# A two-layer hybrid decoder trunk in fp32: when the sums of weight blocks are begun

## The chip, the cores and the metric

One NeuronCore of a Trainium2 chip runs the whole program; the other cores are idle. The metric is the device time of one execution in microseconds (us). The kernel before takes 1888.86 us in the median of three runs (1887.78 to 1890.61).

The engines are named as the profile names them: PE (TensorE, matrix multiply), DVE (VectorE), ACT (ScalarE), POOL (GpSimd), and SP (SyncE), which here issues DMAs only. DMAs of SP run on queue q1, those of POOL on queue q0; both are served by the core's 16 DMA engines.

## The reference

Two layers (DEPTH = 2) of width 2048 over 512 tokens. Each layer projects its input once, hands the columns to three groups of heads, gates their output, projects it back and normalises:

```python
h = jnp.einsum('bsd,dn->bsn', x, w_in)
# split into FoX, DSA and memory parts
y_fox = fox_attention(...) * jax.nn.silu(fg)        # 6 heads, log-forget bias
y_dsa = dsa_attention(...) * jax.nn.silu(dg)        # 6 heads, rotary, top 128 keys by an indexer
y_mem = memory_attention(...) * jax.nn.silu(mg)     # 4 heads into 256 memory tokens
y = jnp.einsum('bsn,nd->bsd', jnp.concatenate([y_fox, y_dsa, y_mem], -1), w_out)
return layer_norm(ALPHA * x + y, ln_gain, ln_bias)
```

The indexer has 16 heads of width 64. All arrays are float32.

## The kernel before

**Products.** Every fp32 matrix product is three matmuls: each operand is split into a high part (rounded to fp32r, made by ACT, tile `whi` for weights) and a low part (the rest, made by DVE, tile `wlo`); high x high, high x low and low x high are added up in PSUM. The weights come from a DRAM tensor `wall` in chunks of 128 x 2048 floats (1 MB), each loaded in two halves of 512 KB into tiles `raw` (seven buffers). A half takes 12 matmuls of 512 columns, or 24 in the kinds with a 128-column result.

**Fewer products.** The large projections are computed in blocks of 2 x 2 by a scheme of seven products (`PRODUCTS`, P1, P7, Q4, P2, Q6, Q5, Q3) instead of eight. Some products need a sum or difference of two weight blocks as their right operand. These come about in four ways:
- The product P7 needs T3, the sum of two blocks. For the value stage T3 of the first pair of columns is summed in DRAM beforehand. For the other five pairs both blocks are loaded (`raw` and four quarter tiles `other` per chunk, 2 MB together) and DVE adds them (`pair_w`, L383).
- Q6 and Q4 need T2 and T4, which grow out of T3 and T2 by adding one more block: in the value stage DVE adds a block that is in SBUF anyway (`make_w`, L404), except for Q4 of the last pair, where an accumulating DMA of POOL adds it to the `raw` tile (`grow_w`, L391). The output stage has accumulating DMAs as well.
- Q5 needs T1, summed in DRAM beforehand for all pairs.
- The output stage needs T3 and T1 of its two pairs, summed in DRAM beforehand.

**The sums in DRAM** are what the change is about. A sum of a block of 1 MB is two DMAs of POOL from DRAM to DRAM: one copies the first block, a later one accumulates the second. "A sum" below means one such DMA; there are 44 per layer (4 for T3 and 24 for T1 of the values, 16 for the output), tile `sum`. They read only the weights. Each is preceded by `pool_waits` (L539): ACT (in the value stage) or DVE (elsewhere) copies one column into `mark`, POOL multiplies it into `seen`. As POOL works in order, the DMA is not issued before ACT or DVE has come to that place of its own order.

**The order of the work** is written out by hand. `stream` (L136) lists the chunks; the main loop (L1615) goes through them and issues, per half, the load of the chunk after next (`load_w`), the split three halves ahead, DVE's sum of a loaded pair four halves ahead, and PE's matmuls. A layer has these stages, named in `now[1]`: memory values and keys (`mv`, `mk`; in layer 1 the stage is called "kv"), the small projection and eight indexer chunks ("index"), then six pairs of value columns ("values"), each of ten chunks in this order (the number is the half of the contraction):

```python
VAL_FIRST = (("P1", 0), ("P7", 0), ("P1", 1), ("P7", 1), ("P2", 0), ("Q6", 0), ("Q6", 1), ("P2", 1),
             ("Q4", 0), ("Q4", 1))
```

After each pair come one or two head chunks (`EARLY_AT`: 1, 1, 1, 1, 2, 2), columns of one head's queries or keys. Then Q5 and Q3 of all pairs with the attention heads between their matmuls ("heads"), and the output stage ("out": 14 steps of two chunks, `place_out[0]` holds the step), whose last step begins the normalisation (`next_x`, L1484).

Side work is written as generators. `tick` (L618) advances each that is due; a generator that yields k is advanced again k ticks later. `all_sums` (L590) is one of them, begun after layer 0's small projection with `whole=True`: it takes no part in the tick at the half of a value or output chunk, so it sees one tick per value or output chunk, at its end, and two per chunk of the other kinds. Where the last step of the output stage ends there is one tick more, just as `next_x` is begun. `paced` (L573) sets the distance between sums: one is issued, then `PACE` = 2 ticks pass, 3 in "out", 1 or 2 in turn in "index"; after a sum issued in "kv" or "heads" it waits until that stage is over. `all_sums` begins layer 1's sums when the stage has become layer 1's.

Of the kernel before, what the change touches and what calls it, by code (L numbers as in the profile page):

```python
# [23 lines left out]
DEPTH = 2  # L24
# [14 lines left out]
PACE = 2  # L39
# [96 lines left out]
def stream():  # L136

    wall = all_chunks()
    where = {c: i for i, c in enumerate(wall)}
    out = []  # L140

    def product(kind, l, name, pair, gs=(0, 1)):
        right = PRODUCTS[name][2]
        for g in gs:
            at = lambda step: where[kind, l, 2 * pair + step[1], 2 * step[0] + g]
            if name in GROWN:
                of, step = GROWN[name]
                src = ("grown", (of, at(step)))
            elif kind == "val" and right == "T3" and pair >= IN_DRAM:
                src = ("pair", tuple(at(step) for step in PAIRED[right]))  # L150
            elif isinstance(right, str):
                src = ("sum", (kind, l, right, pair, g))
            else:
                src = ("wall", at(right))
            out.append(({"val": "vs"}.get(kind, kind), l, (name, pair), g, src))

    for i, c in enumerate(wall):
        kind, l, j = c[:3]
        if kind == "out":
            if c == ("out", l, 0, 0):  # L160
                for name, pair in OUT_ORDER:
                    product("out", l, name, pair)
        elif kind == "val":
            if c == ("val", l, 0, 0):
                early = [x for x in wall if x[1] == l and (x[0], x[2]) in HEAD_CHUNKS]
                for order in (VAL_FIRST, VAL_SECOND):
                    for pair in range(PAIRS):
                        for name, g in order:
                            product("val", l, name, pair, (g,))
                        if order is VAL_FIRST:  # L170
                            for _ in range(EARLY_AT[pair]):
                                x = early.pop(0)
                                out.append((*x, ("wall", where[x])))
        elif (kind, j) not in HEAD_CHUNKS:
            out.append((*c, ("wall", i)))
    return out
# [81 lines left out]
def kernel(  # L258
# [26 lines left out]
    def uid(name):  # L285
        count[0] += 1
        return f"{name}_{count[0]}"
# [16 lines left out]
    def bank(name):  # L304
        return psum.tile([P, 512], F32, tag="b", name=uid(name))
# [25 lines left out]
    chunks = stream()  # L331
# [85 lines left out]
    def last_half(i):  # L417

        return i >= len(chunks) - 4
# [119 lines left out]
    def pool_waits():  # L539

        mark, seen = small("mark", 1), small("seen", 1)
        if now[1] == "values":
            nc.scalar.activation(mark, mhalf, AF.Copy)
        else:
            nc.vector.tensor_copy(mark, mhalf)
        nc.gpsimd.tensor_tensor(seen, mark, mhalf, op=ALU.mult)
# [3 lines left out]
    def block(kind, l, pair, g, step):  # L550
        return wall[where[kind, l, 2 * pair + step[1], 2 * step[0] + g]]

    def add_weights(key, src):
        nc.gpsimd.dma_start(sums[key], src, accum_op=ALU.add, max_dma_last_dim=2 * DM)

    def weight_sums(kind, l, names, pairs, some=(0, 1)):

        for name in names:
            for n in some:
                step = SUM_STEPS[name][n]  # L560
                for pair in pairs:
                    for g in range(2):
                        key = (kind, l, name, pair, g)
                        src = block(kind, l, pair, g, step)
                        pool_waits()
                        if n:
                            add_weights(key, src)
                        else:
                            sums[key] = dram.tile([P, DM], F32, name=uid("sum"))
                            nc.gpsimd.dma_start(sums[key], src, max_dma_last_dim=2 * DM)  # L570
                        yield

    def paced(gen):  # L573

        n = 0
        for _ in gen:
            n += 1
            while now[1] in ("kv", "heads"):
                yield 1
            yield {"out": 3, "index": 1 + n % 2}.get(now[1], PACE)  # L580

    def value_sums(l):

        for n in range(2):
            yield from weight_sums("val", l, ("T3",), range(IN_DRAM), (n,))
        for pair in range(PAIRS):
            for n in range(2):
                yield from weight_sums("val", l, ("T1",), (pair,), (n,))

    def all_sums():  # L590


        for l in range(DEPTH):
            yield from paced(value_sums(l))
            yield from paced(weight_sums("out", l, ("T3", "T1"), range(2)))
            while l + 1 < DEPTH and now[0] == l:
                yield 1

    crow_d = [dram.tile([H_FOX, SEQ], F32, name=f"crow{l}") for l in range(DEPTH)]
# [11 lines left out]
    now = (0, "index")  # L611
# [76 lines left out]
    def drain(done):  # L688

        start = clock.at["PE"]  # L690
        while not done():
            advance()
            if not done():
                clock.at["PE"] += 0.2
            assert clock.at["PE"] < start + 100
# [487 lines left out]
    place_out = [0]  # L1183
# [133 lines left out]
    def load_base(name, pair):  # L1317

        for st in range(2):
            r = st + 2 * (name == "Q5")  # L1320
            assert stored[2 * pair + 1, r] == 1
            t = vraw["base", name, pair, st] = slot("vraw")
            nc.sync.dma_start(t, v_d[2 * pair + 1][r * P:(r + 1) * P, :])
# [114 lines left out]
    def load_res(l, st, dc):  # L1438
        z[st, dc] = slot("z")
        src = x_in if l == 0 else x1_d  # L1440
        nc.gpsimd.dma_start(z[st, dc], src[st * P:(st + 1) * P, dc * 512:(dc + 1) * 512])
# [169 lines left out]
    def ahead_of(i):  # L1611
        return i < len(chunks) and chunks[i][0] == "vs" and chunks[i][2][0] in ("Q5", "Q3")

    first = {l: min(i for i, c in enumerate(chunks) if c[1] == l) for l in range(DEPTH)}
    for i, (kind, l, j, col, _) in enumerate(chunks):  # L1615
        late = last_half(i)
        if kind == "out":
            step = OUT_ORDER.index(j)
            name, pair = j
            if step == col == 0:  # L1620
                now, place_out[0] = (l, "out"), 0
            drain(lambda: (PRODUCTS[name][1], 2 * col + 1) in left)
            chain, aname, _, targets = PRODUCTS[name]
            opens = name in ("P1", "P2", "Q6")
            if col == 0:
                if opens:
                    chains[chain, pair] = [bank("z"), bank("z")]
                zs = chains[chain, pair]

                for st, dc in RES_LOADS.get(step, ()):  # L1630
                    load_res(l, st, dc)
                place_out[0] = step
        elif kind == "vs":
            name, pair = j
            aname = PRODUCTS[name][1]
            opens = name in VAL_OPENS
            if col == 0:
                if opens:
                    chains[VAL_CHAIN[name], pair] = [bank("v"), bank("v")]
            elif ahead_of(i + 1) and 2 * chunks[i + 1][2][1] + 1 not in ROWS:  # L1640
                load_base(*chunks[i + 1][2])
            zs = chains[VAL_CHAIN[name], pair]
        elif kind == "mv":
            if col == 0:
                out_ps = {m: bank("v") for m in range(2)}
        else:
            ps = bank("c")
        for h in range(2):
            n = 2 * i + h
# [134 lines left out]
        if kind == "mv" and l > 0:  # L1784
            now = (l, "kv")
        if kind == "small":
            now = (l, "index")
            stored.clear()
            heads_done.clear()
            memT.clear()  # L1790
            left.clear()
            if l == 0:
                begin(all_sums(), whole=True)
            else:
                begin(residual_rows(l), 2, whole=True)
        if kind == "vs":
            now = (l, "heads" if name in ("Q5", "Q3") else "values")
# [11 lines left out]
        if kind == "out" and step == col == 0:  # L1809
            now = (l, "out")  # L1810
# [100 lines left out]
```

## Time and profile before

| | before |
|---|---|
| median of three runs | 1888.86 us (1887.78 to 1890.61) |
| the profiled execution | 1887.66 us |
| its span, first to last instruction | 1885.8 us |
| PE, DVE, ACT, POOL busy, share of the span | 98%, 85%, 57%, 22% |
| DMA moved | 474.20 MB, mean 251 GB/s |
| SP's queue q1, share of 16 engines' span | 49.3% |
| sums in DRAM: number, median us from issue to landing | 88, 10.5 |
| first and last sum of layer 0; of layer 1, begun at (us) | 70.1 and 509.5; 944.7 and 1448.1 |

In a row of the timeline stand the start in us, the duration in us, the engine, the line, the operation, the tiles (written <- read), how many instructions were merged (x2), and in brackets the idle time ahead of it and what ended it. All operations go through one helper, so every row has its line, L242; tiles tell them apart. SPq and POOLq are the rows of issued DMAs, whose duration is that of the issue, not of the transfer. The chain of waits is the work that ended last, followed back from the end; a row has a start, a duration, and what it was. Rows of stretches (a:b) have busy time and instructions of PE, weight loads, DVE, ACT and POOL, then the granted clock of TensorE, the share of the DMA engines and GB/s. PE's matmuls overlap, so PE is shown busy for longer than it works.

### The profile page before, as it was taken

The page shows a single profiled execution, that of the slowest core. Times are in us where ns is not written, and L with a number is a line of the kernel's source. Part 1 is how long each engine was busy: PE and PEld are TensorE (multiplying, and loading weights), DVE is VectorE, ACT ScalarE, POOL GpSimd, SP SyncE. Part 2 cuts the span into 40 slices and gives each one's busy share as a digit, 9 for nine tenths or more (in the row PEclk, how much of TensorE's full clock was granted, in tenths as well). Part 3 has the DMA queues.
Part 4 walks back from the last instruction along what each step waited for, and adds up shares of the span by engine and source line. Part 5 has one row for each costly group of instructions (what it writes and reads, how often), then busy time and mean ns, then how long its engine had stood idle before and what let it go on. Part 6 is the DMA issues. An engine that isn't in the chain of part 4 may idle for free.

```text
span 1885.8 us, 26424 instructions
## 1 busy us (share of the span) xinstructions
PE 1856.2 (98%) x8994; PEld 1576.5 (84%) x8994; DVE 1608.6 (85%) x2565; ACT 1079.9 (57%) x1752; POOL 410.1 (22%) x587
## 2 busy tenths in 40 slices
PE   9999999999999999999999999999999999999997
PEld 8998888887888888888899978888878888888886
DVE  6789789888789987889898998889787898878898
ACT  5776344444357887555476753454353578875553
POOL 0121222121233211240011221211221343113302
PEclk9999999999999999999999999999999999999999
DMA  9986998897999887986579969977979998879866
GB/s 351 294 239 162 300 303 241 298 273 267 251 244 286 257 220 206 265 210 215 190 256 282 264 173 307 324 235 272 290 266 237 248 299 234 220 215 269 239 215 142
DMA packets 230372, 474.20 MB, mean 251 GB/s; under 512 B 76368, under 2 KB 100944, under 8 KB 229980
## 3 DMA queue, kind: packets, MB, share of 16 engines
q1 hardware_dynamic: 176508, 300.48, 49.3%
q0 software_dynamic: 53152, 170.97, 35.5%
q8 instruction: 71, 1.16, 0.2%
q10 hardware_dynamic: 576, 1.05, 0.2%
q14 instruction: 65, 0.53, 0.1%
HBM read 402.15 MB, written 149.97 MB: 293 GB/s over the span
## 4 chain that ended last, share of the span: by engine, by line
PE 77%; DVE 9%; DMA 7%; ACT 3%; issue 2%; SPq 0%; POOL 0%; DVEq 0%; ACTq 0%; POOLq 0%
PE v L242 38%; PE c L242 17%; PE z L242 14%; DMA other<-in_wall_dram 4%; DVE wlo L242 4%; PE po L242 3%; PE ix L242 1%; PE s L242 1%; DMA grown<-sum 1%; PE pt L242 1%; ACT whi L242 1%; DVE raw L242 1%; DMA raw<-in_wall_dram 1%; DVE acc L242 1%; DVE rope L242 1%
## 5 line engine op out<-in xcount | busy, mean ns | idle before, releaser
L242 ACT ACTIVATE whi<-raw 128x1024 fp32r<-128x1024 f32 (+1 forms) x497 | 521.3, 1056 | 457.4 <-PE v L242 196.4
L242 DVE TENSOR_TENSOR wlo<-raw,whi 128x1024 fp32r<-128x1024 f32 (+1 forms) x497 | 601.7, 1217 | 133.0 <-ACT whi L242 130.5
L242 PE MATMUL v<-whi,vxh 128*128 128x512 f32 x768 | 306.7, 399 | 8.2 <-ACT whi L242 4.7
L242 PE MATMUL v<-wlo,vxh 128*128 128x512 f32 x768 | 302.0, 393 | 5.0 <-DVE wlo L242 5.0
L242 PE MATMUL v<-whi,vxl 128*128 128x512 f32 x768 | 301.4, 392 | 0.0
L242 PE MATMUL v<-whi,xh 128*128 128x512 f32 x576 | 224.4, 390 | 0.0
L242 PE MATMUL v<-wlo,xh 128*128 128x512 f32 x576 | 224.2, 389 | 0.0
L242 PE MATMUL v<-whi,xl 128*128 128x512 f32 x576 | 224.1, 389 | 0.0
L242 PE MATMUL c<-xh,whi 128*128 128x512 f32 (+1 forms) x544 | 197.9, 364 | 0.0
L242 PE MATMUL c<-xh,wlo 128*128 128x512 f32 (+1 forms) x544 | 197.8, 364 | 0.0
L242 PE MATMUL c<-xl,whi 128*128 128x512 f32 (+1 forms) x544 | 197.7, 363 | 0.0
L242 POOL TENSOR_TENSOR seen<-mark,mhalf 128x1 f32<-128x1 f32 x88 | 58.3, 662 | 635.6 <-ACT mark L242 452.6
L242 PEld LDWEIGHTS v<-whi,vxh 128*128 128x128 f32 x768 | 145.1, 189 | 40.2 <-ACT whi L242 7.4
L242 PEld LDWEIGHTS v<-wlo,vxh 128*128 128x128 f32 x768 | 145.3, 189 | 35.5 <-DVE wlo L242 8.5
L242 PEld LDWEIGHTS v<-whi,vxl 128*128 128x128 f32 x768 | 145.1, 189 | 30.8
L242 PE MATMUL z<-wlo,yh 128*128 128x512 f32 (+1 forms) x434 | 167.8, 387 | 2.0 <-DVE wlo L242 2.0
L242 PE MATMUL z<-whi,yh 128*128 128x512 f32 (+1 forms) x434 | 168.6, 389 | 0.0
L242 PE MATMUL z<-whi,yl 128*128 128x512 f32 (+1 forms) x434 | 167.7, 386 | 0.0
L242 PEld LDWEIGHTS v<-wlo,xh 128*128 128x128 f32 x576 | 108.3, 188 | 23.0 <-DVE wlo L242 0.3
L242 PEld LDWEIGHTS v<-whi,xh 128*128 128x128 f32 x576 | 108.4, 188 | 22.6
L242 PEld LDWEIGHTS v<-whi,xl 128*128 128x128 f32 x576 | 108.1, 188 | 22.6
L242 PEld LDWEIGHTS c<-xl,whi 128*128 128x128 f32 x544 | 102.1, 188 | 12.2
(209 smaller groups left out, 3457.9 us busy)
## 6 DMA issues: line engine op xcount, KB each, us to landing
raw<-in_wall_dram SPq DMA_DIRECT2D x331, 512.0 KB, 7.3
sum<-in_wall_dram POOLq DMA_DIRECT2D x88, 1024.0 KB, 10.5
raw<-sum SPq DMA_DIRECT2D x72, 512.0 KB, 7.4
v<-vraw POOLq DMA_DIRECT2D x88, 256.0 KB, 9.2
other<-in_wall_dram SPq DMA_DIRECT2D x80, 256.0 KB, 13.4
vt<-halves POOLq DMA_DIRECT2D x56, 256.0 KB, 9.6
vraw<-v SPq DMA_DIRECT2D x56, 256.0 KB, 5.1
grown<-in_wall_dram POOLq DMA_DIRECT2D x48, 256.0 KB, 8.8
```

The costliest lines, as they stand in the source:

```text
L242: return f(*args, **kw)
```

## The change

Sums are paced otherwise and kept from some places; nothing else changes. `pair_begins` is true while the chunk at hand is no value chunk (a head chunk, in the value stage), the second chunk of Q4, or the first of P1. `paced` now first lets its ticks pass (2 in "out", 3 in "kv", 2 or 3 in turn in layer 1's "index", 1 or 2 in turn in layer 0's; in the values 1 and 2 in turn in layer 0, and 1 after every third sum, else 2, in layer 1), and then, in "heads" or where `pair_begins` holds in the values, waits on, tick by tick. Before, the stage was looked at right after a sum, and only then the ticks passed. It no longer holds in "kv". Layer 1's sums begin at step 9 of layer 0's output stage, not at layer 1's first stage. The number of sums, their order and their operations stay.

```diff
-    def paced(gen):
+    at_chunk = [0]
+
+    def pair_begins():
+
+        kind, _, j, g, _ = chunks[at_chunk[0]]
+        return kind != "vs" or (j[0], g) in (("Q4", 1), ("P1", 0))
+
+    def paced(l, gen):
 
         n = 0
         for _ in gen:
             n += 1
-            while now[1] in ("kv", "heads"):
+            yield {"out": 2, "kv": 3, "index": 1 + n % 2 + l}.get(now[1], PACE - (n % 2 if l == 0 else n % 3 == 0))
+            while now[1] in ("heads",) or now[1] == "values" and pair_begins():
                 yield 1
-            yield {"out": 3, "index": 1 + n % 2}.get(now[1], PACE)
...
         for l in range(DEPTH):
-            yield from paced(value_sums(l))
-            yield from paced(weight_sums("out", l, ("T3", "T1"), range(2)))
-            while l + 1 < DEPTH and now[0] == l:
+            yield from paced(l, value_sums(l))
+            yield from paced(l, weight_sums("out", l, ("T3", "T1"), range(2)))
+            while l + 1 < DEPTH and now[0] == l and (now[1] != "out" or place_out[0] < 9):
                 yield 1
...
     for i, (kind, l, j, col, _) in enumerate(chunks):
         late = last_half(i)
+        at_chunk[0] = i
```

## The prediction

> **What bounds the kernel now.** I read the page first, then the chain of waits in order of time, the waits of TensorE, the timeline at the places that this pointed to, and the share of the DMA engines stretch by stretch.
>
> ```profile
> span 1885.8 us, 26424 instructions
> PE 1856.2 (98%) x8994; PEld 1576.5 (84%) x8994; DVE 1608.6 (85%) x2565; ACT 1079.9 (57%) x1752; POOL 410.1 (22%) x587
> ...
> q0 software_dynamic: 53152, 170.97, 35.5%
> ...
> sum<-in_wall_dram POOLq DMA_DIRECT2D x88, 1024.0 KB, 10.5
> ```
>
> TensorE (PE) is busy nearly all the time, so a change of DMAs can only win where PE stands still or runs at half clock. The chain shows where that is.
>
> ```profile
> 279.89 54.40 PE v L242 x240
> 334.29 10.88 PE c L242 x48
> 390.22 20.61 DMA other<-in_wall_dram
> 410.90 18.73 DMA other<-in_wall_dram
> 469.95 21.76 PE c L242 x96
> ...
> 1271.57 10.88 PE c L242 x48
> 1327.48 21.23 DMA other<-in_wall_dram
> 1348.77 18.62 DMA other<-in_wall_dram
> 1408.55 21.76 PE c L242 x96
> ```
>
> 240 matmuls in 54.40 us are 0.2267 us each, so a value chunk of 24 takes 5.44 us, and a pair (one head chunk of 10.88, ten value chunks) 65.28 us. From the head chunk ahead of pair 3 (334.29) to those ahead of pair 5 (469.95) lie two pairs, 130.56 us by this count and 135.66 by the rows: 5.10 us lost in layer 0. In layer 1 (1271.57 to 1408.55) it is 136.98, so 6.42 lost. In both the chain runs there over two generations of `other` loads, of about 20 us each: the second summands of product P7 of pair 4.
>
> ```profile
> PE v L242 <- ACT whi L242: 4.7, 2, 2.6
> ...
> 429.65 0.69 DVE L242 TENSOR_TENSOR raw<-raw,other 128x512 f32<-128x512 f32 x1 [0.16 <-DMA other<-in_wall_dram]
> ...
> 431.62 0.50 PE L242 MATMUL v<-whi,vxh 128*128 128x512 f32 x1 [2.13 <-ACT whi L242]
> 432.92 0.50 PE L242 MATMUL v<-wlo,vxh 128*128 128x512 f32 x1 [0.80 <-DVE wlo L242]
> ```
>
> The load lands, DVE adds it (429.65), ACT splits the result, and PE has waited 2.13 us for the high part and 0.80 for DVE's low part. The value matmuls wait for ACT's split in two places of the whole run (4.7 us, twice), and these are the two. The rest of the 5.10 us is a slower clock (below). What a sum's place can win stands in these two places, 11.52 us; the other waits in that list hang on work of DVE and ACT, not on a load.
>
> ```profile
> 393.76 0.97 POOL L242 DMA_DIRECT2D sum<-in_wall_dram  x1
> ...
> 401.06 0.89 POOL L242 DMA_DIRECT2D sum<-in_wall_dram  x1
> ...
> 417.39 0.95 POOL L242 DMA_DIRECT2D sum<-in_wall_dram  x1
> ...
> 1338.34 0.89 POOL L242 DMA_DIRECT2D sum<-in_wall_dram  x1
> 1355.25 0.96 POOL L242 DMA_DIRECT2D sum<-in_wall_dram  x1
> ...
> 350.00:370.00 20.00, 20.00 (x90) 16.58 (x89) 17.85 (x25) 9.66 (x13) 2.00 (x4) 1.00 0.70 260
> 390.00:410.00 20.00, 20.00 (x90) 16.58 (x89) 15.92 (x22) 8.08 (x10) 5.50 (x7) 1.00 1.05 293
> 410.00:430.00 20.00, 19.49 (x86) 15.80 (x85) 13.10 (x17) 4.93 (x6) 2.59 (x3) 1.00 1.04 320
> 430.00:440.00 10.00, 7.58 (x25) 5.88 (x26) 9.86 (x13) 7.00 (x10) 1.06 (x2) 0.83 0.51 177
> ...
> 520.00:540.00 20.00, 20.00 (x90) 16.57 (x89) 17.97 (x29) 11.52 (x14) 4.63 (x7) 1.00 1.06 280
> 884.00:930.00 46.00, 46.00 (x205) 38.10 (x204) 39.12 (x55) 23.34 (x27) 0.00 (x0) 1.00 0.64 207
> 930.00:980.00 50.00, 50.00 (x326) 45.35 (x325) 46.93 (x82) 38.33 (x54) 7.35 (x13) 1.00 0.63 198
> 980.00:1000.00 20.00, 20.00 (x116) 18.10 (x115) 14.45 (x19) 6.93 (x9) 2.71 (x5) 1.00 1.03 374
> 1000.00:1010.00 10.00, 10.00 (x61) 9.97 (x60) 6.82 (x13) 7.46 (x13) 0.22 (x1) 1.00 0.79 283
> ```
>
> In the last rows the column before the GB/s is the DMA engines' share. From 390 to 430 us it is full (1.05, 1.04), and three sums are begun in that stretch. So the DMA engines set this stall, and the sums are part of their load.
>
> **What one sum costs the DMA engines.** No row has a sum alone. Queue q0 takes 35.5% of 1885.8 us, 669 us, for 170.97 MB; 88 sums of 1.049 MB are 92.3 MB, 54% of it. By bytes that is 361 us, an estimate of 4.1 us of all 16 engines per sum (88 sums). The median of 10.5 us to landing is the upper bound.
>
> **Part 1, no sum over the pair boundary.** Counting ticks through the stream (one per value or output chunk, two per other chunk) gives, for the old rule, the issue places of the rows above: end of Q4's first chunk, middle of the head chunk, end of P1's first chunk. By the new rule layer 0's output sums begin at P7's first chunk of pair 3 and then stand 1 and 2 chunks apart in turn: P1's second, P2's first, Q6's first, P2's second, Q4's first; the next is due in the head chunk and is held to the end of P7's first chunk of pair 4. With the head chunk at 334.29 + 65.28 = 399.57 the last three are at 388.7 (two chunks ahead of it), 394.1 and 399.57 + 10.88 + 2 x 5.44 = 421.3. So 401.06 and 417.39 go, 8.2 us of DMA work in a full stretch, and one comes in just ahead of it. PE needs the loads 2.93 us sooner (2.13 + 0.80). In layer 1 the new places are P2's second chunk (1326.0) and P7's first (1358.6); 1338.34 and 1355.25 go and nothing takes their place. I take both stalls as gone: -5.10 and -6.42. Without its sums the stretch 390 to 430 holds 41.8 - 12.3 = 29.5 us of work in 40, near the 0.70 of pair 3 at 350 to 370, where PE did not stand. What is late next there is nothing but PE itself. The bounds are 0 and 11.52.
>
> The clock decides how the waits are counted: 430 to 440 was granted 0.83 after a wait of 2.13 us and another of 0.80. The Trainium skill (TensorE: Matmul & The Clock Gate, The HAM clock gate) says that the clock falls to half only after at least one idle window of about 3.4 us. By that page waits this short would cost themselves alone, 2.93 us instead of 5.10 in layer 0; the trace has the slower clock after the shorter wait, and the measurement decides. By the page a wait of 2.5 us in Part 2 would stay 2.5; by the trace it can cost the clock as well.
>
> **Part 2, the last sums of layer 0.** With 1.5 instead of 2 chunks per sum, but held at boundaries, they come later, not sooner: at the ends of P7's first, P1's second, P2's first and Q6's first chunk of pair 5. In pair 5 Q4 is not made by DVE but by accumulating DMAs on POOL's queue, behind the sums.
>
> ```profile
> 521.63 0.88 POOL L242 DMA_DIRECT2D raw<-in_wall_dram  x1 [1.86 <-DVE wlo L242]
> ...
> raw<-in_wall_dram POOLq DMA_DIRECT2D x8, 512.0 KB, 11.8
> ...
> 537.05 1.06 ACT L242 ACTIVATE whi<-raw 128x1024 fp32r<-128x1024 f32 x1
> ...
> 543.23 0.39 PE L242 MATMUL v<-whi,xh 128*128 128x512 f32 x1
> ```
>
> Four such accumulations are issued, one per half chunk, the last at 521.63. The sum of P2's first chunk now enters between the second and the third. The last lands at 521.63 + 11.8 = 533.4; one sum ahead of it on the same queue adds 4.1 (engines to itself) to 10.5 us: 537.5 to 543.9. ACT's split (1.06) and DVE's low part, as long again, end 2.3 us later, 539.8 to 546.2, and PE wants that half at 543.23. So PE waits 0 to 3.0 us; since 520 to 540 is full already (1.06), I take 2.5, near the upper end. With the clock lost as in layer 0 above (5.10 for 2.93) it could reach 5.
>
> **Part 3, layer 1's sums moved forward.** They begin at step 9 of layer 0's output instead of in layer 1's run-in: by the count five from 884 to 930, six from 930 to 980 (one stood there before) and one to 1010, hence 11 more. Work in these 126 us: 0.64 x 46 + 0.63 x 50 + 1.03 x 20 + 0.79 x 10 = 89.4 us, plus 11 x 4.1 = 45.1, so the engines end 8.5 us behind.
>
> ```profile
> 988.71 1.06 ACT L242 ACTIVATE whi<-raw 128x1024 fp32r<-128x1024 f32 x1 [2.99 <-DMA raw<-in_wall_dram]
> ...
> 1000.58 0.42 PE L242 MATMUL c<-xh,whi 128*128 128x384 f32 x1
> ...
> 936.98 2.26 POOL L242 TENSOR_TENSOR rs<-rs,mhalf 128x1 f32<-128x1 f32 x4 [93.89 <-DVE rs L242]
> ...
> 940.04 1.22 DVE L242 TENSOR_TENSOR wlo<-raw,whi 128x1024 fp32r<-128x1024 f32 x1
> ...
> 941.66 0.39 PE L242 MATMUL v<-wlo,memh 128*128 128x512 f32 x1
> ```
>
> The cover is the prefetch: the split that waited for its load at 988.71 is used by PE at 1000.58, 10.8 us after it ends. 8.5 is under that; I take 0.4. The other cost is a queue: one sum is begun in the tick that starts the normalisation, so on POOL its wait and its issue stand ahead of `rs` (936.98), for which DVE's normalising waits, and DVE's next low part follows. DVE ended that at 941.26, PE used it at 941.66, so 0.4 us of cover against about 1 us (an issue alone takes 0.9): 0.6 us. Besides its DMA a sum issues one-column copies on ACT or DVE and on POOL; their number stays 88, and in the values they stay on ACT.
>
> **Sum.** -5.10 - 6.42 + 2.5 + 0.4 + 0.6 = -8.0 us. The profiled execution took 1887.66 us, 1.86 outside its span, so it would become 1879.7; the median of the three runs shown, 1888.86, lies 1.20 above the profiled one, and on it I forecast 1880.9 us.
>
> **Rivals.**
> - Everything new is covered: only the gain counts, 1888.86 - 11.5 = 1877.3. For it: the sum may cost the queue only 4.1 us (539.8 is before 543.23). Against: 1.06 at 520 to 540. Chance 0.16.
> - Layer 0 gives back all it wins: in pair 5 the wait closes the clock gate and costs 5, or pair 4's loads still come late since two sums drain into their first generation (390.22). Then 1888.86 - 6.42 + 1.0 = 1883.4. Chance 0.13.
> - The loads bound the boundary by themselves, or the rule does not keep the sums away there: no change, 1888.9. Against: the 29.5 us of 40 above. Chance 0.05.
> - Slower: the run-in to layer 1 becomes bound by its DMAs. With a price X per sum the engines end 11X - 36.6 us behind at 1010 us; PE stands for what exceeds 10.8. That outweighs the other terms' 8.4 when 11X - 36.6 - 10.8 is over 8.4, from X = 5.1 us on; at 5.6 it is 14.2 - 8.4 = 5.8 us slower, 1894.7. For it: 980 to 1000 is full already (1.03, 374 GB/s). Against: X is 4.1 by the page's q0 row. Chance 0.06.
>
> **How the numbers follow.** The forecast has 0.60; its own range is 1877.5 (Part 2 and 3 covered) to 1884.5 (5 at pair 5, and a few us in the run-in). About 0.2%, 3.8 us, is what a measurement of this kernel can tell from no change, so faster means below 1885.1: forecast, first and second rival, less their tails, 0.84. The same: 0.10. Slower: 0.06. The range 1876.3 to 1885.6 takes in the forecast and the first two rivals.
>
> **What would show it.** Right: no `other` load of about 20 us on the chain ahead of pair 4, 65.3 us per pair there, the two waits for `whi` gone, no half clock at these places; in pair 5 of layer 0 a PE wait of 1 to 3 us in Q4, behind POOL's `raw`; DMA share near 1 from 884 to 1010 with PE unbroken. Wrong: pair 4 still over 66 us, or PE waiting on `whi` between 980 and 1030 for more than 2 us.

## The result, and the profile after

The changed kernel takes 1898.72 us in the median of six runs (1896.82 to 1903.16); the kernel before, run beside it on the same chip, takes 1888.55. The ratio is 1.0055, with a 95% interval of 1.0041 to 1.0069. The forecast was 1880.9 with a range to 1885.6: the kernel became 10 us slower, not 8 faster. The profiled execution took 1903.16 us, the longest of the six, 4.4 above their median, so the profiles of before and after lie 15.5 us apart where the medians lie 10.2.

The page of the changed kernel, the lines that were quoted of before:

```profile
span 1901.4 us, 26428 instructions
PE 1860.0 (98%) x8994; PEld 1579.4 (83%) x8994; DVE 1607.9 (85%) x2572; ACT 1076.7 (57%) x1745; POOL 418.7 (22%) x587
...
q0 software_dynamic: 53152, 170.97, 35.6%
...
sum<-in_wall_dram POOLq DMA_DIRECT2D x88, 1024.0 KB, 9.8
```

Same matmuls, same bytes: the sums were only moved. What grew is the time in which PE stands. TensorE's waits after the change (us in total, times, longest):

```profile
PE ix L242 <- DVE iqs L242: 6.2, 1, 6.2
PE c L242 <- ACT whi L242: 6.0, 1, 6.0
PE v L242 <- DVE wlo L242: 5.4, 7, 1.6
```

The two waits of value matmuls for `whi`, 4.7 us, are gone from the head of this list; two of 6 us stand there (before, in the run-in, the same `ix` waited 0.8 us and no `c` waited for `whi`). Both are matmuls of the run-in to layer 1 (`c`, a memory key chunk; `ix`, the index scores). The chain of waits shows the same exchange:

```profile
336.44 10.88 PE c L242 x48
...
395.75 19.80 DMA other<-in_wall_dram
...
469.74 21.76 PE c L242 x96
...
966.90 15.97 DMA vm<-vh
995.62 8.05 DMA raw<-in_wall_dram
1003.69 22.22 DMA raw<-in_wall_dram
...
1359.07 10.88 PE c L242 x48
1424.35 21.76 PE c L242 x96
```

In layer 1 the pair with the stall now takes 1424.35 - 1359.07 = 65.28 us, exactly the count of its matmuls. In layer 0 two pairs take 133.30, so 2.74 of the 5.10 us are still lost and one `other` load of 20 us is left. New on the chain is the stretch from 967 to 1026: a store of the memory values that takes 16 us, and a load of 512 KB that takes 22.

Stretch by stretch, the rows that answer to those of the prediction:

```profile
884.00:930.00 46.00, 46.00 (x204) 38.10 (x204) 40.06 (x62) 23.31 (x27) 6.29 (x8) 1.00 0.86 262
930.00:980.00 50.00, 50.00 (x309) 44.31 (x308) 39.78 (x73) 30.45 (x42) 20.75 (x18) 1.00 0.90 272
980.00:1000.00 20.00, 12.55 (x77) 12.07 (x77) 14.22 (x21) 10.03 (x14) 4.45 (x8) 0.74 0.73 221
```

The DMA engines were filled from 0.64 and 0.63 to 0.86 and 0.90, and then PE stood: 12.55 busy us of 20 at a granted clock of 0.74. The share of the engines falls in that stretch (0.73, before 1.03), because the loads wait for `raw` tiles that are not split yet. Among SP's waits from 930 to 1050 the longest in total is that of the loads (L373) for DVE's split:

```profile
SPq L373 <- DVE wlo L242: 25.2, 8, 8.1
```

How the first of the two waits comes about is seen in the timeline of POOL, DVE, ACT and PE:

```profile
956.93 8.92 POOL L242 TENSOR_TENSOR seen<-mark,mhalf 128x1 f32<-128x1 f32 x1 [7.58 <-DVE mark L242]
965.80 0.89 POOL L242 DMA_DIRECT2D sum<-in_wall_dram  x1
...
969.99 0.60 POOL L242 DMA_DIRECT2D sum<-in_wall_dram  x1
...
965.73 1.28 DVE L242 TENSOR_TENSOR vl<-v,vh 128x512 fp32r<-128x512 f32 x2
...
978.75 0.78 ACT L242 ACTIVATE xf<-xt,gcol 128x512 f32<-128x512 f32 x1 [7.53 <-DMA vm<-vl]
982.96 0.63 ACT L242 ACTIVATE xh<-xf 128x512 fp32r<-128x512 f32 x1 [3.42 <-DMA vm<-vh]
984.97 1.04 ACT L242 ACTIVATE whi<-raw 128x1024 fp32r<-128x1024 f32 x1
...
986.06 0.58 PE L242 MATMUL c<-memh,whi 128*128 128x256 f32 x1 [6.00 <-ACT whi L242]
```

Two sums are issued within 4.2 us, just as the memory values (`vh`, `vl`) are stored. The stores, 2.3 to 3.9 us in the kernel before, take up to 16. Their tiles come from the same ring of buffers as `xf` and `xh`, the next layer's input, so ACT waits 7.53 and 3.42 us for the stores to end, and the weights' `whi` that PE needs stands behind them in ACT's order. This wait goes with the two sums in nine profiles. Where two are issued 4.2 us apart beside the stores (changed, e2, e11, e12), PE's longest wait there is 4.7 to 6.1 us; with one (e13, e16) it is about 1.75; with none (e3, e6, e18) there is none. The kernels are described below.

The second wait follows from late loads: DVE's split waits for ACT's (4.08 us at 1027), and the index operand `iqs` stands behind DVE's work on `z`.

The starts of the same matmuls in the traces of before and of every kernel below, subtracted from each other, give the change of each stretch (us, + is slower; profiled executions):

| kernel | L0 values to Q4 of pair 5 | Q4, last heads | L0 heads | run-in to L1's values | L1 values to Q4 of pair 5 | Q4 and L1 heads | L1 output |
|---|---|---|---|---|---|---|---|
| changed | -1.7 | +2.2 | +2.2 | +20.4 | -7.8 | +0.2 | +0.2 |
| e1, run-in as before | -2.1 | +1.8 | +2.0 | 0.0 | -6.0 | +12.5 | +11.6 |
| e2, early start alone | -3.8 | 0.0 | +0.1 | +19.1 | -5.4 | +0.1 | +0.4 |
| e3, held in memory stage | -5.2 | +2.0 | +2.0 | +0.3 | -7.7 | +14.0 | +3.2 |
| e5, e1 with marks | -2.4 | +2.8 | +1.9 | +0.8 | -6.7 | +1.2 | +11.2 |
| e6 | -2.6 | +1.9 | +1.9 | +0.1 | -7.8 | +0.2 | +2.9 |
| e7, layer 0's rule alone | -4.9 | +2.4 | +1.9 | +0.1 | +0.5 | 0.0 | -0.6 |
| e8, no rule at boundaries | +1.3 | 0.0 | +0.1 | +0.1 | -7.7 | +0.1 | +0.1 |
| e11, copies | -4.7 | +2.2 | +2.3 | +7.1 | -7.8 | +0.2 | +1.1 |
| e9, nine sums a pair | +13.1 | 0.0 | -0.1 | +0.3 | -7.8 | 0.0 | +1.2 |
| e12, none beside the keys | -3.1 | +1.9 | +1.9 | +9.8 | -7.7 | +9.2 | -0.6 |
| e13, three in memory stage | -5.0 | +1.5 | +1.9 | +5.5 | -7.6 | +8.9 | +0.8 |
| e14, eight a pair | +12.6 | 0.0 | +0.2 | +0.2 | -7.7 | +0.2 | +0.9 |
| e16, none in DVE's burst | -4.7 | +2.5 | +2.1 | +11.1 | -7.7 | +0.2 | +1.3 |
| e18, best | -5.2 | 0.0 | 0.0 | +0.2 | -7.7 | +0.3 | +6.2 |
| e19 | -5.2 | +8.2 | -0.3 | +0.2 | -7.8 | +0.2 | -0.8 |

Not shown are the start up to the first value matmul (+1.5 in the changed kernel, +1.1 in e5, +1.5 in e13, else within 0.2; nothing in it was changed) and layer 0's output stage (within 1.2 throughout). The last column varies between executions. The changed kernel's row is the whole result of its profiled execution: 7.8 and 1.7 are won, 4.4 are given back in layer 0, and 20.4 are lost in the run-in. That loss does not belong to one long execution alone: e2, whose profile lies at its median, loses 19.1 there.

### The profile page after: what moved, and what is told of

Its sections match the earlier page's. It is cut to its first block, busy times and chain, and to the rows that moved or that the text cites. A ratio compares the mean times of both kernels' runs of the same rounds, so it can differ in the third digit from the quotient of the medians.

```text
span 1901.4 us, 26428 instructions
## 1 busy us (share of the span) xinstructions
PE 1860.0 (98%) x8994; PEld 1579.4 (83%) x8994; DVE 1607.9 (85%) x2572; ACT 1076.7 (57%) x1745; POOL 418.7 (22%) x587
## 4 chain that ended last, share of the span: by engine, by line
PE 74%; DVE 11%; DMA 8%; ACT 4%; issue 3%; POOL 0%; SPq 0%; DVEq 0%; ACTq 0%; POOLq 0%
PE v L242 36%; PE c L242 16%; PE z L242 14%; DMA raw<-in_wall_dram 4%; DVE wlo L242 4%; PE po L242 3%; ACT whi L242 1%; PE s L242 1%; PE ix L242 1%; DVE z L242 1%; DVE acc L242 1%; DMA other<-in_wall_dram 1%; PE pt L242 1%; DMA vm<-vh 1%; DVE rope L242 1%
## 5 line engine op out<-in xcount | busy, mean ns | idle before, releaser
L242 POOL TENSOR_TENSOR seen<-mark,mhalf 128x1 f32<-128x1 f32 x88 | 70.5, 801 | 639.9 <-ACT mark L242 332.9
L242 POOL DMA_DIRECT2D v<-vraw x88 | 59.4, 702 | 257.1 <-ACT vraw L242 177.3
```

The source lines that it names most:

```text
L242: return f(*args, **kw)
```

## The experiments

Theory A: the loss is the DMA traffic of layer 1's sums, begun before the index stage. Rival B: it is the small operations ahead of each sum on DVE and POOL. Rival C: the new rule for the values costs as much as it wins. Diffs are against the changed kernel (after) or the kernel before, as said. Ratios are to the kernel before, run on the same chip, with their 95% interval.

**e1, the run-in as before** (against after):

```diff
-            yield {"out": 2, "kv": 3, "index": 1 + n % 2 + l}.get(now[1], PACE - (n % 2 if l == 0 else n % 3 == 0))
+            while now[1] == "kv":
+                yield 1
+            yield {"out": 2, "index": 1 + n % 2}.get(now[1], PACE - (n % 2 if l == 0 else n % 3 == 0))
...
-            while l + 1 < DEPTH and now[0] == l and (now[1] != "out" or place_out[0] < 9):
+            while l + 1 < DEPTH and now[0] == l:
```

> The changed kernel, but layer 1's sums are begun and held in the run-in as in the kernel before (first one in the memory stage, the rest from the index stage on); the new rule for the values stays in both layers. Theory A (the loss is the traffic of layer 1's sums ahead of the index stage): the run-in's 20 us come back, the value stage keeps its gain, 1877 to 1882 us, and no PE wait over 2 us between 970 and 1050. Rival C (the new pace in the values costs as much as the early start): 1888 us or more.

Measured: 1903.67 us, ratio 1.0098 (1.0078 to 1.0119). The run-in's 20 us came back, as theory A has it, and yet the kernel was slower still: the expectation was missed by over 20 us. The reason stands in POOL's sums and PE's waits of this kernel:

```profile
1464.12 0.62 POOL L242 DMA_DIRECT2D sum<-in_wall_dram  x1
1472.38 0.94 POOL L242 DMA_DIRECT2D sum<-in_wall_dram  x1
1725.16 0.91 POOL L242 DMA_DIRECT2D sum<-in_wall_dram  x1
1734.16 0.99 POOL L242 DMA_DIRECT2D sum<-in_wall_dram  x1
1763.75 0.91 POOL L242 DMA_DIRECT2D sum<-in_wall_dram  x1
...
1508.06 0.79 PE L242 MATMUL s<-qh,qh 128*128 128x512 f32 x1 [6.90 <-ACT qh L242]
...
1763.94 1.41 PE L242 MATMUL pt<-ident,pr 128*128 128x128 f32 x5 [5.65 <-ACT pr L242]
```

The rule for the values leaves room for five sums a pair, where six were begun before. Without the early start they are not done by the last pair: the last of the value stage are issued 36 and 44 us ahead of the heads' wait of 6.90 us, and three are left over for the output stage, beside its own loads. The size of the wait at the heads is that of one execution: e5, below, issues the same sums at the same places, and its profile loses 1.2 us there, where e1's loses 12.5. So the early start is not an idle addition: the rule needs it.

**e2, the early start alone** (against before; the values keep their old distance):

```diff
-            while now[1] in ("kv", "heads"):
+            while now[1] == "heads":
                 yield 1
-            yield {"out": 3, "index": 1 + n % 2}.get(now[1], PACE)
+            yield {"out": 2, "kv": 3, "index": 1 + n % 2 + l}.get(now[1], PACE)
...
-            while l + 1 < DEPTH and now[0] == l:
+            while l + 1 < DEPTH and now[0] == l and (now[1] != "out" or place_out[0] < 9):
```

> The kernel before, with only the early start and the new paces of out, memory and index stages; in the values the old distance of 2 and no holding back. Theory A: the same loss in the run-in as in the changed kernel, about 20 us, so 1903 to 1910 us (less where layer 1's pair 4 is spared because its sums have moved forward). Rival C: within 5 us of before, 1884 to 1894.

Measured: 1898.1 us, ratio 1.0065 (1.0047 to 1.0083). The run-in loses 19.1 us with none of the rule in it. The total lies below the range expected, since layer 1's stall at pair 4 is nearly gone here too (-5.4). Why is open. Its sums stand at that place as before: 1346.3, 1353.7, 1370.8 and 1385.5 us, and less the 14.1 us by which this kernel is behind there, that is within 1.5 us of before's 1331.0, 1338.3, 1355.2 and 1371.9. Layer 0's stall shrinks by 3.6 us as well, although nothing in layer 0 is changed up to there. In place of before's waits of 2.13 and 0.80 us its trace has this one:

```profile
430.59 0.50 PE L242 MATMUL v<-wlo,vxh 128*128 128x512 f32 x1 [0.79 <-DVE wlo L242]
```

So with the same sums in the same places the stall at pair 4 is not always there.

**e3, held in the memory stage** (against after):

```diff
-            while now[1] in ("heads",) or now[1] == "values" and pair_begins():
+            while now[1] in ("kv", "heads") or now[1] == "values" and pair_begins():
```

> The changed kernel, with the holding back in the memory stage restored: six sums still begin in layer 0's output stage and one in the memory stage, the others wait for the index stage. Theory A, form 1 (the sums beside the memory chunks and their stores do the harm): 1879 to 1885 us, no PE wait over 2 us between 970 and 1000. Form 2 (the backlog is built up in the output stage already): 1890 us or more, with the wait near 986 still there.

Measured: 1896.57 us, ratio 1.0077 (1.0045 to 1.0108). The run-in loses 0.3: six sums in layer 0's output stage cost nothing, those in the memory stage everything (form 1). But these now come late, as in e1, 17 us go at pair 5, the heads and the output, and the total misses its range.

**e5, only the small operations** (against e1: the copies into `mark` and `seen` at the places of the early sums, no DMA behind them):

```diff
+    def marks():
+        while now[0] == 0 and (now[1] != "out" or place_out[0] < 9):
+            yield 1
+        while now[1] in ("out", "kv"):
+            pool_waits()
+            yield {"out": 2, "kv": 3}[now[1]]
...
                 begin(all_sums(), whole=True)
+                begin(marks(), whole=True)
```

> The late-start kernel with the one-column copies of DVE and POOL that stand ahead of a sum added at the places where the changed kernel begins its early sums (12 or so), without any DMA behind them. Theory A (traffic): within 2 us of the late-start kernel. Rival B (what costs is the place in DVE's and POOL's order, as in the 8.9 us that POOL's copy took near 957): 8 us or more above it.

Measured: 1900.91 us (ratio 1.0078, 1.0056 to 1.0101), 3 below e1 where 2 were allowed, with intervals that overlap; the run-in loses 0.8. POOL's multiply is held up here as well:

```profile
956.02 8.94 POOL L242 TENSOR_TENSOR seen<-mark,mhalf 128x1 f32<-128x1 f32 x1 [7.73 <-DVE mark L242]
```

It harms nobody as long as no DMA stands behind it. Rival B falls.

**e6, the early sums moved out of the memory stage** (against after; e3's hold as well):

```diff
-            yield {"out": 2, "kv": 3, "index": 1 + n % 2 + l}.get(now[1], PACE - (n % 2 if l == 0 else n % 3 == 0))
+            yield {"out": 2, "kv": 3, "index": 1 + n % 2}.get(now[1], PACE - (n % 2 if l == 0 else n % 3 == 0))
...
-            while l + 1 < DEPTH and now[0] == l and (now[1] != "out" or place_out[0] < 9):
+            while l + 1 < DEPTH and now[0] == l and (now[1] != "out" or place_out[0] < 6):
```

> The changed kernel with layer 1's early sums moved out of the memory stage: nine begin in layer 0's output stage from step 6 on, at most one in the memory stage, ten in the index stage at the old distance, and the rule for the values stays, so that the last is issued at product P2 of pair 4 and none is left over. Theory A, second form (the memory stage is the one place where the early sums hurt, and the rule for the values needs the early start so that no sums are left for the output stage): no wait over 2 us from 970 to 1050, none from 1440 to 1520, none at 1750; 1877 to 1883 us. Rival C (the rule for the values costs what it wins): 1885 us or more.

Measured: 1880.89 us, ratio 0.9971 (0.9957 to 0.9984). Without sums in the memory stage the change is 6 us faster than before. That its total is the forecast's is luck: layer 0's terms and layer 1's are not the forecast ones.

**e7, layer 0's rule alone** (against after):

```diff
-            yield {"out": 2, "kv": 3, "index": 1 + n % 2 + l}.get(now[1], PACE - (n % 2 if l == 0 else n % 3 == 0))
-            while now[1] in ("heads",) or now[1] == "values" and pair_begins():
+            while l and now[1] in ("kv", "heads"):
+                yield 1
+            yield {"out": 3, "index": 1 + n % 2}.get(now[1], PACE - (n % 2 if l == 0 else 0))
+            while l == 0 and (now[1] == "heads" or now[1] == "values" and pair_begins()):
                 yield 1
...
-            while l + 1 < DEPTH and now[0] == l and (now[1] != "out" or place_out[0] < 9):
+            while l + 1 < DEPTH and now[0] == l:
```

> The kernel before with the new rule for the values in layer 0 only; layer 1 and the run-in are as before. The prediction's steps for layer 0 give -5.1 + 2.5 = -2.6 us, so 1884. Theory from the trace of after (half of the stall moves to P2 and Q6 of the same pair, Q4 and the heads give back 3 to 4): within 2 us of before, 1885 to 1889.

Measured: 1887.48 us, ratio 1.0004 (0.9990 to 1.0018): nothing in sum. The stretches say why: up to -4.9 at pair 4, +2.4 at Q4 and the head chunks behind it, +1.9 in the heads.

**e8, the early start without any rule at the boundaries** (against before):

```diff
-            yield {"out": 3, "index": 1 + n % 2}.get(now[1], PACE)
+            yield {"out": 2, "index": 1 + n % 2}.get(now[1], PACE)
...
-            while l + 1 < DEPTH and now[0] == l:
+            while l + 1 < DEPTH and now[0] == l and (now[1] != "out" or place_out[0] < 6):
```

> The kernel before with the early start from step 6 of the output stage and the hold in the memory stage, and with the old distance of 2 in the values, nothing held at pair boundaries: its last sum is issued at the end of pair 3. If sums over a pair's boundary are the cause of the stall in layer 1's pair 4 wherever they stand, the one at the end of Q4 still costs 3 to 6 us there: 1884 to 1888. If only the number of sums in flight around pair 4 counts, the stall goes with them: 1878 to 1883, the same as the kernel that holds at boundaries.

Measured: 1879.45 us, ratio 0.9963 (0.9949 to 0.9977). Layer 1 wins the same 7.7 us as with the rule. What cures its pair 4 is that its sums are done by then (the last is issued at 1336.3); keeping them from boundaries adds nothing to that. Beside e6, which has the rule (1880.89 on the same chip, the intervals overlap), the rule wins nothing in sum, as rival C has it for the values.

**e11, copies instead of accumulations** (against after):

```diff
-                        if n:
+                        if n and l and now[1] in ("out", "kv"):
+                            nc.gpsimd.dma_start(sums[key], src, max_dma_last_dim=2 * DM)
+                        elif n:
                             add_weights(key, src)
```

> The changed kernel, but the accumulating sums of layer 1 that begin in the output and memory stages (six or so of twelve) only copy their block, so those T3 and T1 sums lack their first summand. Theory A with the price of an accumulation (5.3 us of the engines against 2.9 for a copy, by the DMA records of these traces): the loss of 20 us in the run-in falls below 10, 1882 to 1890. Rival (any transfer at these places delays the stores and the slots behind them): 1895 or more.

Measured: 1887.7 us, ratio 1.0011 (0.9996 to 1.0025). The same twelve places, six of them cheaper, and the run-in loses 7.1 instead of 20.4: 13.3 us less. That is 2.2 for each of the six; two of them stand in the output stage, where sums cost nothing (e3), so it is 3.3 for each of the four in the memory stage. The DMA records of before and after give the price itself: in sums that had queue q0 to themselves up to their landing, the packets of a copy took 3.0 us of all 16 engines and those of an accumulation 5.8 (medians of 39 and 15). So the loss shrinks by about as much as the DMA work.

**e9, layer 0's sums sooner** (against e8):

```diff
-            yield {"out": 2, "index": 1 + n % 2}.get(now[1], PACE)
+            yield {"out": 2, "index": 1 + n % 2}.get(now[1], PACE - (n % 3 != 0 if l == 0 else 0))
```

> The kernel with the early start and no boundary rule, with layer 0's sums nearer to each other in the values (1, 1 and 2 chunks in turn), so that the last is issued at product P7 of pair 3's boundary chunk Q4 before pair 4, and none stands in pairs 4 and 5. If what counts is that the sums are done before pair 4, the 5 us of layer 0's stall go and nothing comes back at pair 5 or the heads: 1873 to 1877 us. If nine sums per pair fill the DMA engines in pairs 1 to 3, waits of 2 us or more appear there: 1880 or more.

Measured: 1893.76 us, ratio 1.0039 (1.0026 to 1.0051): the second of the two cases. Pair 4 no longer stalls, but pairs 1, 2 and 3 do, at the same place of the pair, the second chunk of P7. The first of these waits:

```profile
233.92 0.66 PE L242 MATMUL v<-whi,vxh 128*128 128x512 f32 x1 [3.04 <-ACT whi L242]
235.18 0.79 PE L242 MATMUL v<-wlo,vxh 128*128 128x512 f32 x1 [0.60 <-DVE wlo L242]
```

It is the signature of before's pair 4. Pairs 1 to 3 go without such a wait with the six sums a pair of before, and not with the eight that the trace shows in pairs 1 and 2 here: the boundary is tender in each of them.

**e14, eight sums per pair, and a hold at pair 4 only** (against e8; `at_chunk` as in after):

```diff
-            yield {"out": 2, "index": 1 + n % 2}.get(now[1], PACE)
+            yield {"out": 2, "index": 1 + n % 2}.get(now[1], PACE - (n % 2 if l == 0 else 0))
+            while 58 <= at_chunk[0] <= 61:
+                yield 1
```

> The kernel with the early start and no boundary rule; in layer 0 the sums are 1 and 2 chunks apart in turn and held only over the boundary of pair 4 (from Q4's first chunk to P1's first); the last four follow within pair 4, and none is in pair 5. If the boundary of pair 4 is the only tender place of layer 0 and the sums beside pair 5's Q4 and the heads are what gave the gain back: 1874 to 1878 us, no wait over 1.5 us in 420 to 545. If the four sums behind the boundary only move the stall to P2 and Q6: 1877 to 1881.

Measured: 1893.85 us, ratio 1.0041 (1.0027 to 1.0055); missed for the same reason, +12.6 in pairs 1 to 3. Pair 4 itself and the heads are clean.

**e12 and e13, fewer sums in the memory stage** (against after; e12 holds in the four key chunks, chunks 141 to 144, e13 spaces the sums out):

```diff
-            while now[1] in ("heads",) or now[1] == "values" and pair_begins():
+            while now[1] == "heads" or 141 <= at_chunk[0] <= 144 or now[1] == "values" and pair_begins():
```
```diff
-            yield {"out": 2, "kv": 3, "index": 1 + n % 2 + l}.get(now[1], PACE - (n % 2 if l == 0 else n % 3 == 0))
+            yield {"out": 2, "kv": 7, "index": 1 + n % 2 + l}.get(now[1], PACE - (n % 2 if l == 0 else n % 3 == 0))
```

> The changed kernel with no sum begun while the four memory key chunks go on (that is, while the four stores of the memory values are out); the three in the memory value chunks stay, the rest moves on by three. If the stores and the slots they hold are the way the harm is done: both waits of about 6 us (986 and 1039) go and the run-in loses under 3 us, 1880 to 1886 us in all. If the amount of DMA work counts, wherever it stands: half the loss stays, 1888 to 1893.

> The changed kernel with a distance of 7 instead of 3 in the memory stage: three sums instead of six, two of them among the memory key chunks, beside the stores. If the amount counts: the same as the kernel with three sums ahead of the stores, loss of the run-in about half. If the place beside the stores counts: one wait of 4 us or more stays near 986, and the run-in loses 5 to 10 us, 1885 to 1892.

Measured: 1897.48 us (ratio 1.0058, 1.0043 to 1.0073) and 1895.64 (1.0047, 1.0032 to 1.0062). In the run-in e12 loses 9.8 and e13 5.5, with three sums each; both lose 9 more at the end of layer 1, since their sums come late. The first wait of e12:

```profile
982.83 0.58 PE L242 MATMUL c<-memh,whi 128*128 128x256 f32 x1 [6.10 <-ACT whi L242]
```

So it does not need a sum placed in the key chunks: the one due in the third value chunk is held by POOL's long multiply and goes out with the next, beside the stores. The wait near 1039 is gone in both. Of e12's two theories neither comes out: the first wait stays whole, the second goes. Of e13's second theory the loss in the run-in comes out (5.5), but not the wait of 4 us or more (the longest there is 1.75) nor the total.

**e16, none in DVE's burst** (against after):

```diff
-            while now[1] in ("heads",) or now[1] == "values" and pair_begins():
+            while now[1] == "heads" or 139 <= at_chunk[0] <= 140 or now[1] == "values" and pair_begins():
```

> The changed kernel with no sum begun in the third and fourth memory value chunk, in which DVE runs the two-input operations of the next layer's input back to back; five sums are still begun in the memory stage, 1.5 chunks apart, instead of six. Theory D (POOL's small multiply is held up there, and the two sums that then go out together delay the stores of the memory values and the slots that ACT needs): no multiply of POOL over 3 us, no wait over 3 us near 983 to 990, the run-in loses under 8 us, below 1889. Theory E (the amount of sums in the memory stage): the run-in loses 15 us or more, 1893 or above.

Measured: 1895.56 us, ratio 1.0044 (1.0028 to 1.0060). No long multiply, no two sums together, and the first wait shrinks:

```profile
981.20 0.38 PE L242 MATMUL c<-memh,whi 128*128 128x256 f32 x1 [1.35 <-ACT whi L242]
983.45 0.39 PE L242 MATMUL c<-memh,wlo 128*128 128x256 f32 x1 [1.74 <-DVE wlo L242]
```

But five sums, none within 6 us of another, still cost 11.1 us. Neither theory as written holds: the bunching (D) makes the first wait long, and the rest goes with the amount (E), by a path that is not shown.

**e18 and e19, the hold at pair 4 alone** (against e8; e18's lines, e19 keeps the old index distance):

```diff
-            yield {"out": 2, "index": 1 + n % 2}.get(now[1], PACE)
+            yield {"out": 2, "index": 1 if l == 0 and n > 4 else 1 + n % 2}.get(now[1], PACE)
+            while 58 <= at_chunk[0] <= 61:
+                yield 1
```

> The kernel with the early start from step 6 and the hold in the memory stage; in layer 0 the fifth and later sums of the index stage follow each other half a chunk apart, the old distance of 2 in the values, held only from Q4's first chunk of pair 3 to P1's first of pair 4; the last sum is issued at the head chunk ahead of pair 5. If the stall of layer 0's pair 4 comes from the sums at that boundary, and the giving back at pair 5 and the heads from the last sums being issued in pair 5: 1873 to 1877 us. If 16 sums in layer 0's index stage are too many: waits of 2 us or more between 80 and 170, 1879 or more.

> As the one before, but with the old distance in layer 0's index stage too, so that the last four sums are issued in pair 5, up to Q4's first chunk or its neighbours. Same theory: the 4 to 5 us of pair 4 are won, 3 to 4 are given back at pair 5 and the heads: 1877 to 1881 us, 2 to 6 above the one before.

Measured: e18 1875.32 us, ratio 0.9944 (0.9927 to 0.9960), faster than both kernels (its profiled execution, with +6.2 in the last stretch, took 1880.13); e19 1882.12, ratio 0.9979 (0.9967 to 0.9990). They win the same 5.2 us at pair 4. Beside e8, which lacks the hold, e18's ratio is 0.0019 lower (some 3.6 us), with intervals that overlap. In e18, whose last sum of layer 0 is issued at 483.21, nothing comes back; in e19, whose last is issued at 536.24, the heads begin with these waits and 8.2 us go (3 to 4 were expected, and the total lies just above its range):

```profile
563.84 0.51 PE L242 MATMUL s<-qh,qh 128*128 128x512 f32 x1 [2.00 <-ACT qh L242]
566.87 0.79 PE L242 MATMUL s<-ql,qh 128*128 128x512 f32 x1 [2.52 <-DVE ql L242]
```

In e18's run-in the engines are full as well, and PE does not stand:

```profile
930.00:980.00 50.00, 50.00 (x345) 46.05 (x344) 48.44 (x81) 37.84 (x53) 8.97 (x16) 1.00 0.81 261
980.00:1000.00 20.00, 20.00 (x103) 18.12 (x103) 12.86 (x20) 7.86 (x13) 2.78 (x6) 1.00 1.04 369
```

## Why the prediction was wrong

The step that failed is Part 3, "layer 1's sums moved forward", taken at +0.4 and measured at +20.4. It set a backlog of the DMA engines against the cover of one load. What PE waited for first was another thing: ACT's split, behind tiles that stores delayed by the sums had not let go. A run-in that is slower by its DMAs was the fourth rival, with a chance of 0.06 and an end of 5.8 us slower; that came true in kind, and larger, but its path over the stores was not named.

- **The backlog.** The sum counted the engines' work from 884 to 1010 against the time in that stretch: 8.5 us behind at its end. That takes all idle time ahead of 980 as usable. But after the change the engines still stayed idle for 0.14 x 46 + 0.10 x 50 = 11.4 us there. Without that time the backlog is an estimated 20 us. That the time can't be used because loads and sums are issued at fixed places is argued, not shown. Nor is the closeness to 20.4 a proof: right behind the first stall, from 985 to 990 us, the engines' share is 0.11: they were not behind there, while the loads waited for tiles. Three sums, not one as counted, were issued from 980 to 1010 (988.90, 998.75, 1009.87).
- **The cover.** 10.8 us were read off one load of the index stage. The memory stage ahead of it has other customers: stores of 2 to 4 us whose tiles ACT uses again, and `x` stores on POOL's queue. In the timeline above the split at 984.97 stands in ACT's order behind the two tiles that waited for stores, so late stores held up every split behind them. There was little cover: e11 took away 13 us of loss with six cheaper DMAs.
- **The price.** 4.1 us a sum is about right as a mean: 3.0 for a copy and 5.8 for an accumulation make 4.4. But four of the six in the memory stage are accumulations: 29 us of the engines there, an estimate from these prices, in place of 25.
- **The places.** e3 and e6: the sums in the output stage are free, at steps 9 and at 6 on. Putting all of the early sums into one sum over 126 us hid that only the memory stage is tight.
- **Part 1 was right in layer 1** (-6.42 foreseen; the values won 7.8, of which 6.4 at pair 4 and 1.4 in the first pair, which the bound of 11.52 had left out), and by the mechanism named: the sums still ran through pair 4, but over its boundary at the foreseen places (1349.7 and 1381.5 us, less the 22.2 by which the kernel is behind there, are 1327.5 and 1359.3; foreseen were 1326.0 and 1358.6), and e1, with the rule and without the early start, wins the same 6.42. e8 shows a second way to it.
- **Part 1 in layer 0** (-5.10 foreseen) came true in part. The change up to Q4 of pair 5 was -1.7 to -5.2 in profiles of kernels whose layer 0 is the same. How much of it is the rule's is not settled: with the sums as before pair 4 lost 5.1 (before), 6.6 (e8) and 1.5 us (e2), with the rule 0 to 3.0, and where only its boundary is kept free or the sums are done sooner (e9, e14, e18, e19) nothing, four times. In the changed kernel's trace half of the stall moved on to P2 and Q6 of the same pair:

```profile
438.48 0.50 PE L242 MATMUL v<-whi,xh 128*128 128x512 f32 x1 [0.52 <-ACT whi L242]
439.74 0.50 PE L242 MATMUL v<-wlo,xh 128*128 128x512 f32 x1 [0.76 <-DVE wlo L242]
...
544.37 0.50 PE L242 MATMUL v<-wlo,xh 128*128 128x512 f32 x1 [0.76 <-DVE wlo L242]
```

- **Part 2 was right in place and half its size**: the last row is the wait in Q4 of pair 5, 0.76 us and 1.25 with the slower matmuls beside it, for 2.5 foreseen. The heads were overlooked: they begin with loads of their own, and the last sum lands at 548.4 us (before at 520.3), with a DMA share of 1.14 from 550 to 560 (before 0.46); +2.2 in the changed kernel. So the second rival, layer 0 giving back all that it wins, came true as well (e7).
- **POOL's `rs`** behind a sum (0.6) cannot be seen in the stretch: the output stage ahead of it changed by -1.0.
- The sign of "wrong" came as named: PE waited on `whi` at 986, for 6.00 us. The row that spoke for this rival, 980 to 1000 at 1.03, was no sign of it: e18 has 1.04 there and PE does not stand.

Open stays how much of the 20 us hangs on the ring of buffers that `vh`, `vl` and `xf` share: giving the stored tiles buffers of their own was not tried. Open is also why the remaining loss of e16 is 11 us and not 5.

## What to carry to other kernels

Free DMA time is counted at the place where a transfer begins and by who waits there, not as a mean over a hundred microseconds: the same sums cost nothing in one stage and over 3 us each (20.4 for six) in the next. Before a transfer is put into a stage, list the small stores in it and whose buffers they free. When a rule keeps work out of some places, count what the rest can carry: with five sums a pair instead of six, three were left over for the output stage (e1).

## What the hardware showed that was not expected

- POOL's multiply of one column took 8.92 us (0.18 to 0.56 in 48 of the other 87 places) while DVE ran TENSOR_TENSOR operations with both inputs in SBUF back to back (`xl<-xf,xh`, `vx<-xf`, `wlo<-raw,whi`, from 956.69). It ended as DVE came to `vl<-v,vh`, whose first input is in PSUM. The Trainium skill (GPSIMD Engine Reference, Specifications) lists POOL's SBUF interfaces as shared with VectorE, in contention with DVE instructions that have two SBUF inputs; the trace agrees, and gives the price when DVE leaves no gap.
- Stores of 256 KB that took 2.3 to 3.9 us took up to 16 when two sums were issued within 4.2 us beside them; when both were copies (e11) up to 9.4; with one sum there (e16) 2.3 to 3.5.
- An accumulating DMA of 1 MB within DRAM took 5.8 us of the 16 engines and a copy of the same size 3.0 (DMA records of before and after).
- PE's loss at pair 4 of layer 0 differs between executions with the same instructions up to there: 0 to 3.0 us among the ten kernels with the new rule, 1.5 to 6.6 among before, e2 and e8. A single profile does not size a stall.
